# Joining the right half's partial products by DMA in a two-layer encoder kernel, with three shifts in ACT's and DVE's queues

## The chip, the cores and the metric

One Trainium2 chip, of which the kernel uses one core. The metric is the device time of one execution in microseconds (us), lower is better. The core has five engines with a queue each, worked off in order: PE (matmuls), DVE (VectorE, elementwise), ACT (ScalarE, elementwise with a function), POOL (GpSimd, here nearly only an issuer of DMAs) and SP (SyncE, the issuer of the weight DMAs). Times before: 2141.31 us, the median of three runs (2138.82 to 2144.55).

## The reference

A trunk of two layers over 256 tokens of width 2048, all in float32. What matters here, cut short:

```python
for l in range(DEPTH):                      # DEPTH = 2
    mod = cond @ w_ada[l] + b_ada[l]        # (2048) @ (2048, 6*2048)
    sh_a, sc_a, g_a, sh_m, sc_m, g_m = split(mod, 6)
    h = _rmsnorm(x) * (1.0 + sc_a) + sh_a
    proj = h @ w_in[l]
    ...                                     # two kinds of attention, out_a and out_b
    mix = concatenate([out_a, out_b]) @ w_o[l]
    x = x + g_a * mix
    h = _rmsnorm(x) * (1.0 + sc_m) + sh_m
    y = square(relu(h @ w_mlp_in[l])) @ w_mlp_out[l]   # D_FF = 4 * 2048
    x = x + g_m * y
return _rmsnorm(x, final_norm_g)
```

## The kernel before

**Numbers in two parts.** A float32 weight tile is split: ACT rounds it to a high half (`hi`, L158), DVE subtracts to get the low half (`lo`, L161). Each product is three matmuls (high by high, high by low, low by high). Activations are split in the same way (`hidh`/`hidl`, `h`). Raw weight tiles (`raw`) come over SP's queue into a ring of seven buffers, which they share with the adaLN weights (`ada`) and the combined weights (`comb`). There are four `hi` and four `lo` tiles.

**adaLN.** Each of the 192 tiles of `w_ada` is 1 MB; DVE multiplies it with the condition and sums (L387, 2.28 us). `more_ada` spreads these over the program: each stage has a rate, and a load is put in when enough credit is there. RATE_K1 is the rate of layer 1's norm stages.

**The MLP of layer 1.** The hidden width is worked off in four blocks (fb = 0 to 3). In a block, the m loop makes 16 tiles of hidden values (`wides`: L224 and L227, their two banks' sums by ACT L1503 and DVE L1504, then relu and square) and at once multiplies them by the left half of `w_mlp_out` (`seven`: seven products of a 2 by 2 scheme with combined weights, L1335 to L1337, which need mixed hidden values, `sh` and `sl`). The right half follows in `right_by_seven`; it needs the mixed values again, which have been stored to HBM (`mixed`, L1172) and are read back (`sr`, L1181). The left half's products are copied from PSUM by ACT (`part`, L353) and added to HBM tiles by POOL's DMAs (`kept`, L1266), one tile for each product. The right half's products are added (L1262) to four HBM tiles for the four output quarters: a product that counts in several quarters is sent once for each (`IN_BLOCKS`), 15 sends for a block. Sends to one tile wait for one another. In the last block, `last_right` computes the right half directly, reads the eight left products and the four right tiles (L1114) back, multiplies the latter by the gate row (`add_rows`: DVE L1119, then a DMA that adds to x, L1120), and finishes with the final norm. The gate row of the MLP is made in that block as well (`gate`: PE transpose, ACT, two DMAs on POOL).

**Rows and squares.** In the output projection and in the last MLP block, the output comes in four columns of 512 (`rows`, L318 to L321). After each, DVE does `yg` (L1425, times the gate row) and `x` (L1427), and ACT squares x for the next norm (`squares`, L1441).

**Queries and values.** In layer 1's attention, `up_q` makes queries and copies them on ACT (`qn`, L353), `up_v` splits the value weights `w_uv`; the scores (L1676) need the queries.

**What sets the order.** A list scheduler gives each engine its order: among the instructions whose inputs it holds to be ready it takes the one written first. So an instruction may stand in a queue far ahead of its place in the code, and once there it holds up all behind it until its inputs are there. Temporary tiles of 128 by 512 (hidden values, mixed values, copies, sums) come out of one pool of 40 buffers (`u`).

Of the kernel before, what the change touches and what calls it, by code (L numbers as in the profile page):

```python
# [69 lines left out]
def consts():  # L70
# [24 lines left out]
WHOLE = 6  # L95


RATE_A0, RATE_V, RATE_A1, RATE_A2, RATE_K, RATE_K1, RATE_M0 = 1.1, 1.6, 0.7, 1.0, 0.6, 0.4, 1.0
RATE_M3 = 0.75
RATE_S, RATE_R, RATE_E = (0.1, 0.2), (0.8, 0.2), 0.0  # L100
RAWS = 7
IN_BLOCKS = {
    1: ((0, 2), (0, 3), (1, 2), (1, 3)), 2: ((0, 2),), 3: ((0, 3),), 4: ((1, 2),),
    5: ((0, 3), (1, 3)), 6: ((0, 3), (1, 2), (1, 3)), 7: ((1, 2), (1, 3)), 8: ((1, 3),),
}
FILL = "0|1|2|3||||rlm"


class Trunk:
# [213 lines left out]
    def rows(self, src, xs, c, last=False):  # L323

        pss = [self.bank("pr") for _ in range(2)]
        for kq in range(2 if last else 4):
            if last and kq == 1:
                self.first_squares()
            self.rows_by_k(pss, self.weights(src[c, kq]), xs, kq)
        if last:  # L330
            self.quiet = True
            w = [self.weights(src[c, kq]) for kq in (2, 3)]
            for t in range(2):
                for kq in (2, 3):
                    self.rows_by_k(pss, w[kq - 2], xs, kq, (t,))
        return pss
# [13 lines left out]

    def copy(self, ps, name, scale=1.0):
        t = self.u(name)
        self.nc.scalar.activation(t, ps, AF.Copy, scale=scale)  # L353
        return t


# [61 lines left out]
    def setup(self):  # L418
        nc, io, cp = self.nc, self.io, self.cp
        self.ada_plan()  # L420
        self.cond = cp.tile([P, D], F32, name="cond")
        ck = cp.tile([P, NK], F32, name="ck")
        self.pos = cp.tile([P, T + 8], I32, name="pos")
        self.vec = cp.tile([P, NVEC], F32, name="vec")
        self.K = cp.tile([P, NCONST], F32, name="K")
        for t, name, q in ((ck, "ck", nc.scalar), (self.vec, "vec", nc.sync), (self.pos, "pos", nc.scalar),
                           (self.K, "consts", nc.sync)):
            q.dma_start(t, io[name])
        xt = [[None, None], [None, None]]
        for h in range(2):  # L430
            for t in range(2):
                xt[t][h] = self.wp.tile([P, D // 2], F32, tag=("hi", "lo")[h], name=self.name("xt"), bufs=4)
                q = nc.scalar if (h, t) == (1, 0) else nc.sync
                ins = q.dma_start(xt[t][h], io["x"][t, :, D // 2 * h : D // 2 * h + D // 2])
                if q is nc.scalar:
                    issued = ins
        self.eps = cp.tile([P, 1], F32, name="eps")
        nc.gpsimd.memset(self.eps, EPS)
        self.ones = cp.tile([P, P], F32, name="ones")
        nc.gpsimd.memset(self.ones, 1.0)  # L440
        self.ident = cp.tile([P, P], F32, name="ident")
        make_identity(nc, self.ident)
        self.behind(nc.scalar.activation(ck, ck, AF.Silu), issued)
        nc.scalar.activation(self.s("root", 1), ck[:, :1], AF.Sqrt, bias=self.eps, scale=0.0)
        for j in range(4):
            c = slice(512 * j, 512 * j + 512)
            ps = self.bank("pc").rearrange("p a b -> p (a b)")
            for i in range(4):
                col = ck[:, 4 * j + i : 4 * j + i + 1].broadcast_to([P, P])
                nc.tensor.transpose(ps[:, i * P : i * P + P], col, self.ident)  # L450
            if j % 2:
                cond_dve = nc.vector.tensor_copy(self.cond[:, c], ps)
            else:
                cond_act = nc.scalar.activation(self.cond[:, c], ps, AF.Copy)
        self.bias_setup(cond_dve, cond_act)
        self.x = cp.tile([P, NK, T], F32, name="x")
        self.xr = self.x.rearrange("p (a b) c -> p a (b c)", a=2)
        tot = self.sp.tile([P, 2, 2], F32, tag="s22", name="xsq")
        for h in range(2):
            for t in range(2):  # L460
                junk = self.bias[:, 2 * t : 2 * t + 2].rearrange("p a b c -> p (a b c)")
                ins = nc.scalar.activation(junk, xt[t][h], AF.Square, accum_out=tot[:, h, t : t + 1])
                self.behind(ins, cond_act)

        def turn(n, after=None, later=False):
            h, p = n // 4, n % 4
            ps = self.bank("px")
            for i in range(2):
                c = (2 * p + i) * P
                for t in range(2):  # L470
                    nc.tensor.transpose(ps[:, i, t * P : (t + 1) * P], xt[t][h][:, c : c + P], self.ident)
            k = 8 * h + 2 * p

            def copy(after):
                ins = nc.scalar.activation(self.x[:, k : k + 2], ps, AF.Copy)
                if after is not None:
                    self.behind(ins, after)

            return copy if later else copy(after)

        return tot, turn
# [407 lines left out]
    def layer(self, l, acc=None):  # L889
# [28 lines left out]
        else:  # L918
            cqr = [self.joined(banks[i : i + 2], self.u("cqr")) for i in (0, 2)]
            ckr = self.joined(banks[4:], self.u("ckr"))  # L920
        q = []
        cq, ckv = [], []
        kk, qn, kn, qr, vm, a, at, v, o = [], [], [], [], [], [], [], [], []
        self.mo = []
# [17 lines left out]

        def up_q(b):
            qn.extend(self.copy(ps, "qn", ms) for ps in self.small(io["w_uq"][l, b], cq, 4))

        def up_r():
            if l:
# [3 lines left out]
            qr.extend([self.rope_q(x)] * 2 for x in raw)  # L951

        def up_v():
            w = self.weights(io["w_uv"][l])
            for cg in range(2):
                pss = [self.bank("pv") for _ in range(2)]
                self.tokens_by_k(pss, [[z[:, 512 * cg : 512 * cg + 512] for z in y] for y in w], ckv, True, True)
                vm.append([self.copy(ps, "vm") for ps in pss])
# [163 lines left out]
    def block_by_seven(self, l, fb, h, banks):  # L1122
# [2 lines left out]
        hid, pairs, sums, stored = [], [], [None] * 7, {}  # L1125
        plain = len(banks)
        end = fb == NFB - 1
        self.rate = RATE_S[l]
        for m in range(0, plain, 2):
            hid += self.relu2(self.joined(banks[m : m + 2], self.t("sum")))  # L1130
        for m in range(plain, NK, 2):
            both = self.t("sum")
            for j in range(2):
                src = io["w_m11"][NK * fb + m + j - 6] if l else io["w_m10"][NK * fb + m + j - 12]
                ps = self.wides([src], h)[0]
                self.join(ps, both[:, j])
                if len(pairs) > 1:
                    pairs[-2][j]()
            r = self.relu(both)
            parts = self.split(r, "hid")  # L1140
            hid += parts
            mixed = self.mixed(r)
            if l and not end and m >= NK // 2:
                stored[m // 2] = self.stored(mixed)
            pairs.append(self.seven(io[f"w_ms{l}"][fb, m // 2], parts, mixed, sums, m == plain, m == NK - 2))
            if end and m == 2:
                self.gate(l, 5)
        for pair in pairs[-2:]:
            for f in pair:
# [35 lines left out]
    def right_by_seven(self, fb, hid, plain, stored, light):  # L1185
# [9 lines left out]
        begun = [[self.bank("pr") for _ in range(2)] for _ in range(2)]  # L1195
        mixed = {}
        n = NK // 4
        for q in range(n):
            if q > 1:
                mixed[n + q - 2] = self.again(stored[n + q - 2])  # L1200
            self.both_by_k(self.weights(io["w_mr"][fb, q]), hid, 2 * q, begun, q == n - 1, False)
            if light:
                light.pop(0)()
        for f in light:
            f()
        self.keep_product(8, begun[1][1])
        sums = [None, begun[0][0], begun[1][0], begun[0][1], None, None, None]
        for q in range(n, 2 * n):
            if q + 2 < 2 * n:
                mixed[q + 2] = self.again(stored[q + 2])  # L1210
            parts = hid[2 * q : 2 * q + 2]
            for f in self.seven(io["w_mr"][fb, q], parts, mixed[q], sums, q == n, q == 2 * n - 1, (2, 3, 4)):
                f()
        for i in (1, 2, 3, 5, 7, 6, 4):
            self.keep_product(i, sums[i - 1])

    def keep_product(self, i, ps):

        t = self.copy(ps, "part")
        for z in IN_BLOCKS[i]:  # L1220
            self.keep_tile(z, t)

    def last_right(self, hid, sums):

# [6 lines left out]
            for i in group:  # L1231
                op(acc[i], sums[i - 1], acc[i], ALU.add)

        def rows(c):
            for t in range(2):
                self.add_rows(acc[t, c], t, c)

        light = [
            lambda: add(3, 5), lambda: add(7, 6, 4), lambda: rows(2),
            lambda: halves.extend(self.merged(acc)), lambda: rows(3),  # L1240
            lambda: done(halves[0], 0), lambda: done(halves[1], 1),
        ]
        self.read_kept(acc, list(range(1, 9)) + [(t, c) for c in (2, 3) for t in range(2)])
        add(1, 2)
        pss = [self.bank("pr") for _ in range(2)]
        for kq in range(4):
# [182 lines left out]
    def updates(self, pss, c, last=False):  # L1429

        for t in range(2):
            self.update(pss[t].rearrange("p a b -> p (a b)"), t, c)
            if last:
                self.squares(t, c)

    def squares(self, t, c):

# [361 lines left out]
```

## Time and profile before

| | us |
|---|---|
| median of three runs | 2141.31 |
| the profiled execution's own time | 2141.52 |
| its span, first to last instruction | 2139.6 |
| granted TensorE clock | 0.999 |

Where the time goes, by stage; PE and DVE are busy times from a table by windows:

| stage | from to (us) | length | PE busy | DVE busy |
|---|---|---|---|---|
| layer 0: output projection | 325 to 400 | 75 | 73.05 | 64.79 |
| layer 1: attention norm | 1100 to 1147 | 47 | 45.77 | 44.77 |
| layer 1: output projection | 1340 to 1441 | 101 | 101.00 | 81.43 |
| layer 1: MLP norm | 1441 to 1480 | 39 | 38.76 | 37.30 |
| MLP block 0 | 1480 to 1614 | 134 | 134.00 | 121.58 |
| block 1: m loop | 1614 to 1742 | 128 | 126.61 | 114.71 |
| block 1: right half | 1742 to 1789 | 47 | 44.38 | 39.28 |
| block 2: m loop | 1789 to 1916 | 127 | 126.89 | 109.77 |
| block 2: right half | 1916 to 1959 | 43 | 42.70 | 37.22 |
| block 3: m loop | 1959 to 2087 | 128 | 128.00 | 110.89 |
| last right half and final norm | 2087 to 2139 | 52 | 44.24 | 45.46 |

A row of a timeline reads: start, duration, engine, line, operation, output and input tile, and in brackets the idle time ahead of it and what ended it. A row of waits reads: engine, tile, line, what it waited for, then the total, the number of times and the longest. An engine that is busy all the time in a stage sets that stage's length; idle time of another engine costs nothing by itself.

### The profile page before, as it was taken

To read this page: it belongs to the slowest core of one execution; us is meant where nothing else is said; L and a number is where in the kernel's file an instruction comes from. 1 tells how busy PE (TensorE), PEld (TensorE's weight loads), DVE (VectorE), ACT (ScalarE), POOL (GpSimd) and SP (SyncE) were. 2 spreads that over 40 slices of the span, in tenths; PEclk is the share of its full clock that TensorE was granted. 3 is DMA by queue.
4 is the path that set the end of the run, shared out by engine and by line. 5 is a ranking of instruction groups with operands and counts; after the bars stand their busy time and mean duration, and the time that the engine had idled before them with its cause. 6 is when DMAs were issued, how large, how long until landed. Compare 5 with 4: busy or idle time off the path is not lost.

```text
span 2139.6 us, 30063 instructions
## 1 busy us (share of the span) xinstructions
PE 2107.5 (98%) x11327; PEld 1821.2 (85%) x11327; DVE 1854.9 (87%) x2515; ACT 1287.6 (60%) x1904; POOL 136.1 (6%) x202
## 2 busy tenths in 40 slices
PE   7999999999999999999999999999999999999998
PEld 6899888898888888888889998888888888888886
DVE  8889888989799888879978897889988997898898
ACT  6555663564466566646454576647667666676674
POOL 0000000000000100111000000000022022012110
PEclk9999999999999999999999999999999999999999
DMA  9999898789965965899978877877689699679864
GB/s 396 423 386 341 320 352 352 283 316 405 383 218 189 372 226 211 296 404 381 388 261 319 305 288 282 298 302 266 225 309 324 223 302 285 224 228 311 252 228 148
DMA packets 110674, 643.04 MB, mean 301 GB/s; under 512 B 12800, under 2 KB 13248, under 8 KB 43712
## 3 DMA queue, kind: packets, MB, share of 16 engines
q1 hardware_dynamic: 85536, 586.41, 72.0%
q0 software_dynamic: 24272, 53.52, 10.2%
q8 instruction: 88, 1.44, 0.3%
q10 hardware_dynamic: 720, 1.19, 0.2%
q14 instruction: 58, 0.48, 0.1%
HBM read 602.25 MB, written 35.68 MB: 298 GB/s over the span
## 4 chain that ended last, share of the span: by engine, by line
PE 89%; DVE 4%; DMA 4%; issue 2%; ACT 1%; POOL 0%; SPq 0%; ACTq 0%; DVEq 0%; POOLq 0%
PE ps L224 19%; PE ps L227 10%; PE pr L318 7%; PE pr L321 7%; PE pr L319 7%; PE pp L1336 3%; PE pp L1337 3%; PE pp L1335 3%; PE pk L267 3%; DMA ada<-in_w_ada 2%; PE pk L201 2%; PE pk L205 2%; PE pk L204 2%; DVE lo L161 2%; PE pk L291 2%
## 5 line engine op out<-in xcount | busy, mean ns | idle before, releaser
L158 ACT ACTIVATE hi<-raw 128x1024 fp32r<-128x1024 f32 (+2 forms) x714 | 707.1, 1003 | 469.5 <-PE pr L319 127.2
L161 DVE TENSOR_TENSOR lo<-raw,hi 128x1024 fp32r<-128x1024 f32 (+2 forms) x714 | 807.7, 1150 | 175.7 <-ACT hi L158 107.3
L387 DVE SCALAR_TENSOR_TENSOR ada<-ada,cond 128x2048 f32<-128x2048 f32 x192 | 438.3, 2285 | 13.8 <-DMA ada<-in_w_ada 12.8
L224 PE MATMUL ps<-h,hi 128*128 128x512 f32 x1856 | 442.1, 391 | 0.9 <-DVE sum L1504 0.4
L224 PEld LDWEIGHTS ps<-h,hi 128*128 128x128 f32 x1856 | 343.8, 188 | 77.5 <-DVE sum L1504 6.7
L227 PEld LDWEIGHTS ps<-h,lo 128*128 128x128 f32 x1856 | 236.4, 191 | 8.1
L227 PE MATMUL ps<-h,lo 128*128 128x256 f32 x1856 | 238.9, 283 | 0.0
L318 PE MATMUL pr<-hi,hidh 128*128 128x512 f32 x448 | 174.4, 389 | 0.1
L319 PE MATMUL pr<-hi,hidl 128*128 128x512 f32 x448 | 174.3, 389 | 0.0
L161 DVE TENSOR_TENSOR lo<-comb,hi 128x1024 fp32r<-128x1024 f32 x114 | 138.8, 1220 | 8.0 <-ACT hi L158 3.6
L158 ACT ACTIVATE hi<-comb 128x1024 fp32r<-128x1024 f32 x114 | 120.2, 1055 | 30.3 <-PE pp L1337 12.3
L321 PE MATMUL pr<-lo,hidh 128*128 128x512 f32 x448 | 111.4, 389 | 0.0
L318 PEld LDWEIGHTS pr<-hi,hidh 128*128 128x128 f32 x448 | 84.1, 188 | 18.0 <-ACT hi L158 0.5
L321 PEld LDWEIGHTS pr<-lo,hidh 128*128 128x128 f32 x448 | 84.0, 188 | 17.6 <-DVE lo L161 0.2
L319 PEld LDWEIGHTS pr<-hi,hidl 128*128 128x128 f32 x448 | 84.1, 188 | 17.4
L201 PE MATMUL pk<-h,hi 128*128 128x256 f32 x320 | 90.4, 285 | 0.2 <-ACT h L722 0.2
L205 PE MATMUL pk<-h,lo 128*128 128x256 f32 x320 | 90.5, 283 | 0.0
L204 PE MATMUL pk<-h,hi 128*128 128x256 f32 x320 | 90.5, 283 | 0.0
L1262 POOL DMA_DIRECT2D kept<-part x76 | 67.0, 989 | 332.0 <-ACT part L353 257.4
L1503 ACT ACTIVATE sum<-ps 128x256 f32<-128x256 f32 x110 | 41.8, 383 | 75.5 <-PE ps L227 74.3
L267 PE MATMUL pk<-hf,w 128*128 128x256 f32 x384 | 83.9, 379 | 0.0
L267 PEld LDWEIGHTS pk<-hf,w 128*128 128x128 f32 x384 | 72.6, 190 | 10.2 <-ACT hf L694 0.4
(307 smaller groups left out, 3844.3 us busy)
## 6 DMA issues: line engine op xcount, KB each, us to landing
ada<-in_w_ada SPq DMA_DIRECT2D x192, 1024.0 KB, 7.5
raw<-in_w_m SPq DMA_DIRECT2D x166, 1024.0 KB, 7.5
raw<-in_w_ms SPq DMA_DIRECT2D x48, 1024.0 KB, 6.2
raw<-in_w_o SPq DMA_DIRECT2D x32, 1024.0 KB, 7.1
kept<-part POOLq DMA_DIRECT2D x100, 256.0 KB, 9.2
raw<-in_w_mr SPq DMA_DIRECT2D x24, 1024.0 KB, 6.4
raw<-in_w_m SPq DMA_DIRECT2D x24, 768.0 KB, 5.8
raw<-in_w_dv SPq DMA_DIRECT2D x16, 1024.0 KB, 5.0
```

The source lines that it names most:

```text
L158: ins = self.nc.scalar.activation(hi, v, AF.Copy)
L161: ins = self.nc.vector.tensor_tensor(lo, v, hi.bitcast(F32), ALU.subtract)
L201: ins = mm(ps, hi, x[0], start=first, stop=False, skip_group_check=shared)
L204: mm(ps, hi, x[1], start=False, stop=False, skip_group_check=shared)
L205: self.last_mac = mm(ps, lo, x[0], start=False, stop=last, skip_group_check=shared)
L224: mm(ps.rearrange("p a b -> p (a b)"), part(w, k, 0), x[2], start=k == 0, stop=False)
L227: mm(ps[:, 0], part(w, k, 1), x[0], start=False, stop=k == nk - 1)
L267: self.nc.tensor.matmul(ps, v, whole[k], start=first, stop=last, skip_group_check=True)
L318: mm(ps, xh[:, c], part(i, 0), start=kq == 0 and i == 0, stop=False)
L319: mm(ps, xl[:, c], part(i, 0), start=False, stop=False)
L321: self.last_mm = mm(ps, xh[:, c], part(i, 1), start=False, stop=kq == 3 and i == 3)
L387: ins = nc.vector.scalar_tensor_tensor(w, w, 1.0, self.cond, ALU.mult, ALU.mult, accum_out=acc[:, i : i + 1])
```

## The change

- The right half's eight products get HBM tiles of their own (`("r", i)`): 8 sends for a block instead of 15, and no two of a block to one tile.
- At the start of block 3, `right_steps` reads these eight tiles into SBUF, and eight DMAs on POOL add one SBUF tile to another (`IN_ORDER`, L1225 of the changed program). Then the four quarters are multiplied by the gate row and added to x, in the code at m = 12 and 14 of block 3 instead of in `last_right`.
- The last pair of mixed values of a block stays in SBUF: 6 instead of 8 stores and reads for a block, and the reads are written one step earlier.
- The gate row is made in block 2 instead of block 3.
- RATE_K1 goes from 0.4 to 0.3.
- In the output projection and the last MLP block the squares of x of columns 0 to 2 are written behind the second weights of the next column.
- In layer 1, the split of the value weights is written behind the first copy of the queries.

```diff
--- before.py
+++ after.py
-RATE_A0, RATE_V, RATE_A1, RATE_A2, RATE_K, RATE_K1, RATE_M0 = 1.1, 1.6, 0.7, 1.0, 0.6, 0.4, 1.0
+RATE_A0, RATE_V, RATE_A1, RATE_A2, RATE_K, RATE_K1, RATE_M0 = 1.1, 1.6, 0.7, 1.0, 0.6, 0.3, 1.0
...
-IN_BLOCKS = {
-    1: ((0, 2), (0, 3), (1, 2), (1, 3)), 2: ((0, 2),), 3: ((0, 3),), 4: ((1, 2),),
-    5: ((0, 3), (1, 3)), 6: ((0, 3), (1, 2), (1, 3)), 7: ((1, 2), (1, 3)), 8: ((1, 3),),
-}
+IN_ORDER = ((6, 1), (2, 1), (7, 6), (4, 7), (6, 5), (3, 6), (5, 7), (5, 8))
...
         for kq in range(2 if last else 4):
+            w = self.weights(src[c, kq])
+            if kq == 1:
+                self.late_squares()
             if last and kq == 1:
                 self.first_squares()
-            self.rows_by_k(pss, self.weights(src[c, kq]), xs, kq)
+            self.rows_by_k(pss, w, xs, kq)
...
         def up_q(b):
             qn.extend(self.copy(ps, "qn", ms) for ps in self.small(io["w_uq"][l, b], cq, 4))
+            after_queries.append(self.last_copy)
...
         def up_v():
-            w = self.weights(io["w_uv"][l])
+            w = self.weights(io["w_uv"][l], order=(after_queries[0], None) if l else None)
...
         end = fb == NFB - 1
+        right = self.right_steps() if l and end else []
...
                     pairs[-2][j]()
+                if m and right and (len(right) > 4 or m >= NK - 4):
+                    right.pop(0)()
...
             if l and not end and m >= NK // 2:
-                stored[m // 2] = self.stored(mixed)
+                stored[m // 2] = mixed if m == NK - 2 else self.stored(mixed)
...
-            if end and m == 2:
+            if l and fb == NFB - 2 and m == 2:
                 self.gate(l, 5)
...
+        mixed[2 * n - 1] = stored[2 * n - 1]
         for q in range(n):
-            if q > 1:
-                mixed[n + q - 2] = self.again(stored[n + q - 2])
+            if q:
+                mixed[n + q - 1] = self.again(stored[n + q - 1])
...
-        self.keep_product(8, begun[1][1])
+        self.keep(("r", 8), begun[1][1])
         sums = [None, begun[0][0], begun[1][0], begun[0][1], None, None, None]
         for q in range(n, 2 * n):
-            if q + 2 < 2 * n:
-                mixed[q + 2] = self.again(stored[q + 2])
...
         for i in (1, 2, 3, 5, 7, 6, 4):
-            self.keep_product(i, sums[i - 1])
-
-    def keep_product(self, i, ps):
-
-        t = self.copy(ps, "part")
-        for z in IN_BLOCKS[i]:
-            self.keep_tile(z, t)
+            self.keep(("r", i), sums[i - 1])
+
+    def right_steps(self):
+
+        acc = {}
+        self.read_kept(acc, [("r", i) for i in (1, 6, 2, 7, 4, 5, 3, 8)])
+        add = lambda i, j: self.nc.gpsimd.dma_start(acc["r", i], acc["r", j], accum_op=ALU.add)
+        out = {2: (0, 2), 4: (1, 2), 3: (0, 3), 5: (1, 3)}
+        return [lambda p=p: add(*p) for p in IN_ORDER] + [
+            lambda i=i, tc=tc: self.add_rows(acc["r", i], *tc) for i, tc in out.items()]
...
-        def rows(c):
-            for t in range(2):
-                self.add_rows(acc[t, c], t, c)
-
...
-        self.read_kept(acc, list(range(1, 9)) + [(t, c) for c in (2, 3) for t in range(2)])
+        self.read_kept(acc, range(1, 9))
...
             self.update(pss[t].rearrange("p a b -> p (a b)"), t, c)
-            if last:
+            if last and c == 3:
                 self.squares(t, c)
+            elif last:
+                self.later.append((t, c))
+
+    def late_squares(self):
+
+        for t, c in self.later:
+            self.squares(t, c)
+        self.later = []
```

`copy` also notes its last instruction (`last_copy`), and `setup` begins with an empty list `later`.

What this does to the queues is shown at three places. Lines shift by a few: L1119 of before is L1121, L1120 is L1122, L1504 is L1514, L1345 to L1347 are L1347 to L1349, L161 is L158 (the low half), L727 is L728 and L719 is L720.

**DVE, block 3, second step of the m loop.** `sum` is the sum behind a wide, `comb` the combined weights and mixed values, `lo` a low half, `acc` a tile with the right half's joined products. Before:

```order
L1504 SCALAR_TENSOR_TENSOR sum_18327<-ps_18328,sum_18327 128x256
L161 TENSOR_TENSOR lo_18450<-raw_18443,hi_18449 128x1024
L1320 TENSOR_TENSOR sl_18324<-comb_18318,sh_18323 128x512
L1345 TENSOR_TENSOR comb_18646<-raw_18644 128x1024
L1346 TENSOR_TENSOR comb_18646<-raw_18644,comb_18646 128x512
L161 TENSOR_TENSOR lo_18501<-raw_18494,hi_18500 128x512
L161 TENSOR_TENSOR lo_18508<-raw_18494,hi_18507 128x1024
L1504 SCALAR_TENSOR_TENSOR sum_18327<-ps_18373,sum_18327 128x256
L1347 TENSOR_TENSOR comb_18646<-raw_18644,comb_18646 128x512
L1314 TENSOR_TENSOR comb_18425<-relu_18418 128x128
L1315 TENSOR_TENSOR comb_18425<-relu_18418 128x128
L1316 TENSOR_TENSOR comb_18425<-comb_18425,relu_18418 128x128
```

The same place in the changed program:

```order
L1347 TENSOR_TENSOR comb_18625<-raw_18623 128x1024
L1121 TENSOR_TENSOR acc_18194<-acc_18194,bias 128x512
L158 TENSOR_TENSOR lo_18478<-raw_18471,hi_18477 128x512
L158 TENSOR_TENSOR lo_18485<-raw_18471,hi_18484 128x1024
L1514 SCALAR_TENSOR_TENSOR sum_18309<-ps_18356,sum_18309 128x256
L1348 TENSOR_TENSOR comb_18625<-raw_18623,comb_18625 128x512
L1121 TENSOR_TENSOR acc_18198<-acc_18198,bias 128x512
L1349 TENSOR_TENSOR comb_18625<-raw_18623,comb_18625 128x512
L1121 TENSOR_TENSOR acc_18196<-acc_18196,bias 128x512
L1316 TENSOR_TENSOR comb_18409<-relu_18402 128x128
L1317 TENSOR_TENSOR comb_18409<-relu_18402 128x128
L1318 TENSOR_TENSOR comb_18409<-comb_18409,relu_18402 128x128
```

Three of the four multiplies stand here, though the code has them at m = 12 and 14; the first stands ten rows earlier, directly behind the sum of the second wide of the block (that of 1972.18 us in the trace of before). Nothing else in DVE's order differs here.

**POOL, start of block 3.** Before, the queue ends its 15 sends of block 2 here and goes on with the gate row:

```order
L1262 DMA kept_14968<-part_18212 128x512
L1262 DMA kept_14970<-part_18217 128x512
L1262 DMA kept_14778<-part_18212 128x512
L1414 DMA gate_18434<-modT_18436 16x128
L1416 DMA bias<-gate_18434 128x2048
```

In the changed program the sends are followed by eight reads (tiles 18186 to 18200 hold products 1, 6, 2, 7, 4, 5, 3, 8 in this order; the first needs product 1, the second product 6, the fifth product 4, which is the block's last send), and then:

```order
L1225 DMA acc_18188<-acc_18186 128x512
L1225 DMA acc_18190<-acc_18186 128x512
L1225 DMA acc_18192<-acc_18188 128x512
L1122 DMA x<-acc_18190 128x512
L1225 DMA acc_18194<-acc_18192 128x512
L1225 DMA acc_18188<-acc_18196 128x512
L1225 DMA acc_18198<-acc_18188 128x512
L1225 DMA acc_18196<-acc_18192 128x512
L1122 DMA x<-acc_18194 128x512
L1225 DMA acc_18196<-acc_18200 128x512
L1122 DMA x<-acc_18198 128x512
L1122 DMA x<-acc_18196 128x512
```

Each L1225 adds the tile on the right to that on the left. The multiplies above read 18190, 18194, 18198 and 18196, so each stands behind the L1225 rows that write its tile.

**DVE, MLP norm of layer 1.** `ht` and `h` make the normed input, `lo` the weights' low halves. Before:

```order
L161 TENSOR_TENSOR lo_13452<-raw_13445,hi_13451 128x768
L719 SCALAR_TENSOR_TENSOR ht_13481<-xT_13286,mod_95,pn_13247 128x256 x2
L161 TENSOR_TENSOR lo_13493<-raw_13490,hi_13492 128x768
L727 SCALAR_TENSOR_TENSOR h_13482<-ht_13481,mod_93,h_13482 128x256
L161 TENSOR_TENSOR lo_13497<-raw_13490,hi_13496 128x768
L727 SCALAR_TENSOR_TENSOR h_13483<-ht_13481,mod_93,h_13483 128x256
L387 SCALAR_TENSOR_TENSOR ada_13455,macc_98<-ada_13455,cond 128x2048
```

The changed program:

```order
L158 TENSOR_TENSOR lo_13451<-raw_13444,hi_13450 128x768
L387 SCALAR_TENSOR_TENSOR ada_13409,macc_98<-ada_13409,cond 128x2048
L720 SCALAR_TENSOR_TENSOR ht_13479<-xT_13282,mod_95,pn_13243 128x256 x2
L158 TENSOR_TENSOR lo_13491<-raw_13488,hi_13490 128x768
L158 TENSOR_TENSOR lo_13495<-raw_13488,hi_13494 128x768
L728 SCALAR_TENSOR_TENSOR h_13480<-ht_13479,mod_93,h_13480 128x256
L728 SCALAR_TENSOR_TENSOR h_13481<-ht_13479,mod_93,h_13481 128x256
```

The `ada` stands five instructions earlier, and both low halves stand ahead of the first `h`.

More of the change, by code (lines that the diff above doesn't have):

```diff
@@ L352, in copy @@
         t = self.u(name)
-        self.nc.scalar.activation(t, ps, AF.Copy, scale=scale)
+        self.last_copy = self.nc.scalar.activation(t, ps, AF.Copy, scale=scale)
         return t
@@ L920, in layer @@
             ckr = self.joined(banks[4:], self.u("ckr"))
-        q = []
+        q, after_queries = [], []
         cq, ckv = [], []
@@ L1232, in add @@
                 op(acc[i], sums[i - 1], acc[i], ALU.add)
-        def rows(c):
-            for t in range(2):
-                self.add_rows(acc[t, c], t, c)
         light = [
-            lambda: add(3, 5), lambda: add(7, 6, 4), lambda: rows(2),
-            lambda: halves.extend(self.merged(acc)), lambda: rows(3),
+            lambda: add(3, 5), lambda: add(7, 6, 4), lambda: halves.extend(self.merged(acc)),
             lambda: done(halves[0], 0), lambda: done(halves[1], 1),
         ]
-        self.read_kept(acc, list(range(1, 9)) + [(t, c) for c in (2, 3) for t in range(2)])
+        self.read_kept(acc, range(1, 9))
         add(1, 2)
@@ L1432, in updates @@
             self.update(pss[t].rearrange("p a b -> p (a b)"), t, c)
-            if last:
+            if last and c == 3:
                 self.squares(t, c)
+            elif last:
[3 more added lines that the diff above has]
+            self.squares(t, c)
+        self.later = []
     def squares(self, t, c):
```

## The prediction

> **What bounds the kernel now.** The page's first part comes first, then the waits of PE.
>
> ```profile
> PE 2107.5 (98%) x11327; PEld 1821.2 (85%) x11327; DVE 1854.9 (87%) x2515; ACT 1287.6 (60%) x1904; POOL 136.1 (6%) x202
> PE pr L1337 <- DMA sr<-mixed: 2.8, 3, 1.3
> PE pr L318 <- ACT hi L158: 1.9, 2, 1.0
> PE psm L1676 <- ACT qn L353: 1.3, 1, 1.3
> PE pk L291 <- DVE h L727: 1.0, 2, 0.5
> PE pp L1335 <- ACT hi L158: 0.9, 1, 0.9
> ```
>
> PE works 98% of the span, so no more than about 32 us of 2139.6 can be won without removing matmuls, and the change removes none. The wait rows give us in total, times, and the longest. The five rows are those the change can reach, 7.9 us together. DVE at 87% is nearly full, and its queue is strictly in order: whatever stops DVE for longer than its lead over PE stops PE. So each part is judged by two questions: does one of these waits go, and does DVE get a new one?
>
> **The change, part by part.** *Squares later (layer 0, output projection).* A high half (ACT, L158) comes late because ACT stands behind a square that waits for DVE's x, and DVE does an adaLN sum (`ada`) between yg and x:
>
> ```profile
> 350.15 2.28 DVE L387 SCALAR_TENSOR_TENSOR ada<-ada,cond 128x2048 f32<-128x2048 f32 x1
> 352.35 0.69 DVE L1427 TENSOR_TENSOR x<-x,yg 128x512 f32<-128x512 f32 x1
> 353.07 0.63 ACT L1441 ACTIVATE sq<-x 128x512 f32<-128x512 f32 x1 [9.50 <-DVE x L1427]
> 355.04 3.89 ACT L158 ACTIVATE hi<-raw 128x1024 fp32r<-128x1024 f32 x4
> ```
>
> In the changed order ACT's queue is the same here, but DVE does yg, yg, x, x, then the low halves, then `ada`. The squares start about 2.2 us earlier and the wait of `pr L318` goes: −1.9. Elsewhere (layer 0's last block, layer 1's output projection) the low halves now stand behind yg and x, where PE waits for nothing today. Each yg or x ahead of a low half delays it by 0.6 to 0.7 us (the row of 352.35), most of which is slack, as no wait of PE stands there: +0.3 for all six places, bounds 0 and 1.2.
>
> *One `ada` load fewer in layer 1's norm stages.* In the attention norm the second `ada` no longer stands ahead of `h`:
>
> ```profile
> 1127.07 2.28 DVE L387 SCALAR_TENSOR_TENSOR ada<-ada,cond 128x2048 f32<-128x2048 f32 x1
> 1131.47 1.67 PE L291 MATMUL pk<-h,hi 128*128 128x512 f32 x6 [0.53 <-DVE h L727]
> ```
>
> That is −0.5. In the MLP norm it moves the wrong way: from behind an `h` to ahead of one (the order rows of the MLP norm above).
>
> ```profile
> 1457.03 0.86 DVE L719 SCALAR_TENSOR_TENSOR ht<-xT,mod,pn 128x256 f32<-128x256 f32 x2
> 1457.81 0.95 DVE L161 TENSOR_TENSOR lo<-raw,hi 128x768 fp32r<-128x768 f32 x1
> 1458.68 0.48 DVE L727 SCALAR_TENSOR_TENSOR h<-ht,mod,h 128x256 fp32r<-128x256 f32 x1
> 1460.88 1.55 PE L291 MATMUL pk<-h,hi 128*128 128x512 f32 x6
> ```
>
> At 1457.03 DVE now does `ada` (2.2 net), two ht (0.8), two lo (0.87 each), then h (0.48): ready at 1462.3 for a matmul that starts at 1460.88. **+1.4**, bounds 0 and 1.6.
>
> *Query copies ahead of the value weights.* ACT fills all its high halves, then the query copy, and PE's scores wait for that copy:
>
> ```profile
> 1270.21 1.06 ACT L158 ACTIVATE hi<-raw 128x1024 fp32r<-128x1024 f32 x1 [0.88 <-PE pv L305]
> 1271.18 1.07 ACT L353 ACTIVATE qn<-pss 128x512 f32<-128x512 f32 x2
> ```
>
> The copies now come first: −1.3.
>
> *Right half kept apart; last mixed pair stays in SBUF.* Today three reloads stand on POOL's queue behind the partial sum of product 8, which waits 9.4 us for ACT:
>
> ```profile
> 1768.75 0.89 POOL L1262 DMA_DIRECT2D kept<-part  x1 [9.41 <-ACT part L353]
> 1769.32 1.95 POOL L1181 DMA_DIRECT2D sr<-mixed  x3
> ```
>
> In the changed order all reloads stand ahead of it and the last pair is not stored at all: the wait of `pr L1337` goes, −2.8. The stores fall from 15 to 8 per block; nothing but POOL and the u buffers waits for these.
>
> *More `ada` in blocks 0 and 1.* An `ada` directly ahead of the sum that frees the psum bank, with PE drawn to a high half that is not ready, stands once in today's m loops:
>
> ```profile
> 1717.30 2.28 DVE L387 SCALAR_TENSOR_TENSOR ada<-ada,cond 128x2048 f32<-128x2048 f32 x1
> 1719.55 0.50 PE L1335 MATMUL pp<-hi,hidh 128*128 128x512 f32 x1 [0.92 <-ACT hi L158]
> ```
>
> The changed order has the same PE, ACT and DVE sequence twice (blocks 0 and 1): one more, +0.9, bounds 0 and 2. The last `ada` and the gate row at the start of block 2 lie where DVE has idle time (2.32 us in the row of 1974.92 below, one block later).
>
> These terms sum to −1.9 + 0.3 − 0.5 + 1.4 − 1.3 − 2.8 + 0.9 = **−3.9**.
>
> *The sums joined by DMA, and where DVE waits for them.* This is the largest term. DVE's four multiplies L1121 stand among the first steps of block 3 (the order rows of block 3 above), each behind a DMA. Today DVE and PE pass there at:
>
> ```profile
> 1972.18 0.42 DVE L1504 SCALAR_TENSOR_TENSOR sum<-ps,sum 128x256 f32<-128x256 f32 x1
> 1974.92 0.29 DVE L1314 TENSOR_TENSOR comb<-relu 128x128 f32<-128x128 f32 x1 [2.32 <-ACT relu L1512]
> 1985.85 0.29 DVE L1314 TENSOR_TENSOR comb<-relu 128x128 f32<-128x128 f32 x1 [1.57 <-ACT relu L1512]
> 1986.92 1.22 DVE L161 TENSOR_TENSOR lo<-comb,hi 128x1024 fp32r<-128x1024 f32 x1
> 1989.70 0.39 PE L1336 MATMUL pp<-lo,sh 128*128 128x512 f32 x1
> ```
>
> The first multiply comes right after the sum of 1972.18, the fourth right before the comb of 1985.85; the lo of 1986.92 is needed by PE at 1989.70. When are their inputs there? The partial sums of block 2 leave at the same time as now:
>
> ```profile
> 1956.28 3.58 POOL L1262 DMA_DIRECT2D kept<-part  x4 [12.76 <-ACT part L353]
> 1965.89 0.88 POOL L1262 DMA_DIRECT2D kept<-part  x1 [6.03 <-DMA kept<-part]
> kept<-part POOLq DMA_DIRECT2D x4, 256.0 KB, 12.9
> kept<-part POOLq DMA_DIRECT2D x1, 256.0 KB, 12.4
> acc<-kept POOLq DMA_DIRECT2D x2, 256.0 KB, 2.9
> acc<-kept POOLq DMA_DIRECT2D x8, 256.0 KB, 12.9
> x<-acc POOLq DMA_DIRECT2D x4, 256.0 KB, 3.3
> x<-acc POOLq DMA_DIRECT2D x3, 256.0 KB, 12.0
> ```
>
> The last six rows are DMA issues, with the median us from issue to landing: the four stores of 1956.28, the one of 1965.89, the first two and the next eight reads for the last right half (from 2061.07 and 2074.83), the four x additions after 2098 and the three of 1036.37. The queue is shared with the weight stream, and the same 256 KB takes 2.9 us when that is quiet and 12 us when it is not. Today the fifth store lands at 1965.89 + 12.4 = 1978.3. It is queued without a gap, so the sixth and seventh of the changed kernel land near 1979.6 and 1981 (1.3 us apart, an estimate: POOL needs 0.9 for one, a quarter of the 3.58, and the weight stream thins out by then). The reads of products 6 and 4 wait for exactly these two. Eight reads at about 0.55 us each put the first accumulate at **1984**.
>
> From there DVE's fourth multiply is five accumulates deep (6+=1, 7+=6, then 4+=7 with 5 into 6 beside it, 5+=7, 5+=8), and POOL issues each only when the one before has landed. No SBUF-to-SBUF accumulate between two work tiles is in this trace; the nearest row is x<-acc, 3.3 us quiet, 12.0 loaded. I take 3.3, since a DVE that stands still frees no weight buffers and so stops the weight stream, plus 0.6 until POOL's next issue (1965.89 comes that long after its landing). Five links of 3.9 and 1.8 for the issues in between give 21.3: the fourth input is there at 2005.3. The multiply (0.6), the rest of the comb (0.8) and the lo (1.2) follow, so PE gets at 2007.9 what it used at 1989.70: **+18.2** of PE standing still. In general the stall is the start of the chain minus 1965.8. Nothing makes it up later, since PE is the bound, and it can't be negative, since PE waits for nothing there today.
>
> The bounds: with a queue as quiet as the 2.9 row from 1956 on, the stores land by 1964.6, the chain starts at 1967.5 and the stall is 1.7; with links of 5 us in place of 3.3, it is 27.
>
> Sum: 2141.5 (the profiled execution's own time, 2139.6 of span and 1.9 around it) − 3.9 + 18.2 = 2155.8. That execution is 0.2 above the median of the runs shown, so **2155.5**.
>
> The Trainium skill, "DMA: Bandwidth & Descriptors", section on the anatomy of one DMA on the SWDGE path, fits one such transfer as 2.0 us plus bytes over 436 KB per us, 2.6 us for 256 KB. By that rule the links would be 3.2 and no store late, the stall would vanish and the sum would be 2137.4, the near end of the first rival. The trace disagrees: 2.9 us at best, 12.9 beside the weight stream; the same page's section on SWDGE, HWDGE and iDMA says that an engine serves the two kinds of queue in turn, which fits the loaded rows.
>
> **The rivals.** (1) *Quiet queue*, the case that ends not slower: the change halves the stores on this queue, so the sums may be joined nearly by the time DVE asks. The price is 0 to 6: 2137 to 2143. For it: the 2.9 and 3.3 rows. Against: those come where few weights are streamed, and the 12.9 row comes at this very place. It decides if the chain starts before about 1972; from 1976 on the stall outweighs the gains by over 0.3%. (2) *Slow links*: weights already under way keep the queue loaded; 2164. (3) *All small waits go and DVE waits for none*: quiet queue, no new stall at the norm (+1.4) or by `ada` (+0.9): 2141.3 − 6.5 + 0.3 = 2135.1, and 0.1 less for each of the nine waits gone, as the matmul behind one is longer (0.50 at 1719.55, 0.39 at 1989.70): 2134.2. (4) *The squares do nothing*, ACT's order there being unchanged: 1.9 more, inside the range of each case.
>
> **How the numbers follow.** Forecast (2148 to 2160) 0.55; slow links 0.12; quiet queue 0.24, of which 0.03 comes out above 2148; all waits gone 0.09, three quarters of it under 2134.9. A measurement of this kernel can tell about 0.3%, 6.4 us, from no change. So faster 0.07, same 0.23, slower 0.70. The range takes in most of the quiet case and nearly all of the slow one: 2138 to 2164; the forecast's own is 2148 to 2160.
>
> **What would show it.** In the profile of the changed kernel: DVE's L1121 in block 3 with idle time ahead of it that ends with a DMA, PE waiting for DVE's lo some 10 us later, L1225 rows on POOL about 4 us apart, and a slice of low PE near 1985 to 2005. Gone: the waits on sr, on qn, and L318's on hi. New: a short wait of L291 for h near 1461, and a second one of L1335. If L1121 has no idle time ahead of it, the forecast is wrong by its whole largest term.

## The result, and the profile after

| | us |
|---|---|
| before, median of five runs (2138.71 to 2144.55) | 2140.37 |
| after, median of five runs (2169.34 to 2175.14) | 2171.86 |
| ratio | 1.0145, 95% interval 1.0128 to 1.0161 |
| profiled execution after: own time, span, granted clock | 2172.9, 2171.1, 0.991 |

The change costs 31.5 us; about 14 were predicted (2155.5 against 2141.3), and 2171.86 lies above the range. The busy row of the page, the waits of PE and the waits of DVE for a DMA (in all, times, longest), all of the changed kernel:

```profile
PE 2115.3 (97%) x11327; PEld 1827.7 (84%) x11327; DVE 1853.5 (85%) x2515; ACT 1284.9 (59%) x1904; POOL 118.9 (5%) x181
PE pp L1338 <- DVE lo L158: 18.8, 4, 12.8
PE ps L224 <- DVE lo L158: 8.6, 2, 8.4
PE pp L1337 <- ACT hi L155: 1.8, 2, 0.9
PE pk L288 <- DVE h L728: 1.7, 2, 1.3
DVE acc L1121 <- DMA acc<-acc: 29.5, 3, 18.7
```

The waits on `sr`, on `qn` and of the output projection on `hi` are gone. In their place stand 27.4 us of PE waiting for low halves of DVE (L1338 and L224), of which 21.2 fall in block 3 (8.38 and 12.79 in the rows below). DVE itself waits 29.5 us at L1121. DVE does the same work as before (1853.5 us against 1854.9) in a longer span: it lost time standing. POOL's timeline shows the chain it stood behind (start, duration, line, operation, tiles, count, idle before):

```profile
1961.81 4.42 POOL L1264 DMA_DIRECT2D kept<-part  x5 [0.15 <-issue]
1982.96 3.92 POOL L1116 DMA_DIRECT2D acc<-kept  x7 [14.22 <-DMA kept<-part]
1986.86 1.85 POOL L1225 DMA_DIRECT2D acc<-acc  x2
1993.60 0.85 POOL L1225 DMA_DIRECT2D acc<-acc  x1 [4.88 <-DMA acc<-acc]
1997.09 1.77 POOL L1225 DMA_DIRECT2D acc<-acc  x2 [0.62 <-DMA acc<-acc]
2003.84 1.80 POOL L1225 DMA_DIRECT2D acc<-acc  x2 [4.98 <-DMA acc<-acc]
2013.16 0.87 POOL L1225 DMA_DIRECT2D acc<-acc  x1 [6.63 <-DMA acc<-acc]
```

From one link's issue to the next: 6.7, 3.5, 6.8 and 9.3 us. DVE, SP and PE at the same place:

```profile
1975.39 0.42 DVE L1514 SCALAR_TENSOR_TENSOR sum<-ps,sum 128x256 f32<-128x256 f32 x1
1994.52 0.69 DVE L1121 TENSOR_TENSOR acc<-acc,bias 128x512 f32<-128x512 f32 x1 [18.72 <-DMA acc<-acc]
1999.41 4.37 SPq L174 DMA_DIRECT2D raw<-in_w_m  x2
2011.44 0.69 DVE L1121 TENSOR_TENSOR acc<-acc,bias 128x512 f32<-128x512 f32 x1 [7.08 <-DMA acc<-acc]
2016.45 0.69 DVE L1121 TENSOR_TENSOR acc<-acc,bias 128x512 f32<-128x512 f32 x1 [3.72 <-DMA acc<-acc]
1997.13 2.07 PE L224 MATMUL ps<-h,lo 128*128 128x256 f32 x8 [8.38 <-DVE lo L158]
2019.07 0.80 PE L1338 MATMUL pp<-lo,sh 128*128 128x512 f32 x1 [12.79 <-DVE lo L158]
2019.66 0.63 PE L1339 MATMUL pp<-hi,sl 128*128 128x512 f32 x1
```

The matmul that PE reached at 1989.70 before is now reached at 2019.07, 29.4 us later. Of this 3.2 had been lost earlier (the sum of 1972.18 stands at 1975.39), so block 3's wait costs 26.2, and the slow matmuls behind it more (0.63 us each; they took 0.39 before). The matmuls between the two waits are slow as well (a granted clock of 0.50 from 1996 to 2004), but that costs nothing extra: DVE stands for the chain behind them, until 2011.44 and again until 2016.45.

Two stalls that nobody forecast made the earlier loss. In block 2's right half:

```profile
1923.65 0.60 ACT L353 ACTIVATE part<-pp 128x512 f32<-128x512 f32 x1 [4.95 <-DMA kept<-part]
1926.25 1.23 DVE L158 TENSOR_TENSOR lo<-raw,hi 128x1024 fp32r<-128x1024 f32 x1 [4.92 <-ACT hi L155]
1940.88 1.23 DVE L1347 TENSOR_TENSOR comb<-raw 128x1024 f32<-128x1024 f32 x1 [2.73 <-DMA raw<-in_w_mr]
1944.02 0.50 PE L1338 MATMUL pp<-lo,sr 128*128 128x512 f32 x1 [3.48 <-DVE lo L158]
1944.73 0.63 PE L1337 MATMUL pp<-hi,sr 128*128 128x512 f32 x1
```

ACT's copy waits for the landing of a send, that is, for a free `u` buffer; DVE waits for ACT, the next load of these weights goes out late, and PE stands 3.48 us. SP's issues of the two loads, first in the changed kernel and then in the kernel before:

```profile
1920.76 13.55 SPq L174 DMA_DIRECT2D raw<-in_w_mr  x2
1922.02 8.95 SPq L177 DMA_DIRECT2D raw<-in_w_mr  x2
```

The second load ends its issue at 1934.3 instead of 1931.0.

At the start of block 2, SP's queue, DVE and PE:

```profile
1772.08 0.33 SPq L371 DMA_DIRECT2D ada<-in_w_ada  x1
1793.21 0.33 SPq L1371 DMA_DIRECT2D cond<-in_fg  x1
1795.92 0.33 SPq L174 DMA_DIRECT2D raw<-in_w_ms  x1
1811.82 1.22 DVE L1347 TENSOR_TENSOR comb<-raw 128x1024 f32<-128x1024 f32 x1 [3.75 <-DMA raw<-in_w_ms]
1818.31 0.50 PE L1338 MATMUL pp<-lo,sh 128*128 128x512 f32 x1 [2.10 <-DVE lo L158]
```

The last `ada` tile is now loaded between the first weights of block 2; a weight lands late, and PE stands 2.10 us.

### The profile page after: what moved, and what is told of

It reads as the page before. It is cut to its first block, busy times and chain, and to the rows that moved or that the text cites. A ratio compares the mean times of both kernels' runs of the same rounds, so it can differ in the third digit from the quotient of the medians.

```text
span 2171.1 us, 30006 instructions
## 1 busy us (share of the span) xinstructions
PE 2115.3 (97%) x11327; PEld 1827.7 (84%) x11327; DVE 1853.5 (85%) x2515; ACT 1284.9 (59%) x1904; POOL 118.9 (5%) x181
## 3 DMA queue, kind: packets, MB, share of 16 engines
q8 instruction: 89, 1.46, 0.3%
## 4 chain that ended last, share of the span: by engine, by line
PE 82%; issue 8%; DVE 4%; DMA 4%; ACT 1%; POOL 1%; SPq 0%; POOLq 0%; DVEq 0%; ACTq 0%
PE ps L221 15%; PE ps L224 8%; PE pr L315 7%; PE pr L316 7%; PE pr L318 7%; PE pk L264 3%; PE pp L1338 3%; PE pp L1339 3%; PE pp L1337 3%; PE pk L198 2%; PE pk L202 2%; PE pk L201 2%; DVE lo L158 2%; PE pv L302 2%; PE pv L300 2%
## 5 line engine op out<-in xcount | busy, mean ns | idle before, releaser
L158 DVE TENSOR_TENSOR lo<-raw,hi 128x1024 fp32r<-128x1024 f32 (+2 forms) x714 | 807.4, 1150 | 187.0 <-ACT hi L155 110.0
L387 DVE SCALAR_TENSOR_TENSOR ada<-ada,cond 128x2048 f32<-128x2048 f32 x192 | 438.2, 2284 | 13.2 <-DMA ada<-in_w_ada 12.2
L224 PEld LDWEIGHTS ps<-h,lo 128*128 128x128 f32 x1856 | 238.0, 192 | 17.4 <-DVE lo L158 9.3
L224 PE MATMUL ps<-h,lo 128*128 128x256 f32 x1856 | 241.1, 284 | 8.6 <-DVE lo L158 8.6
L158 DVE TENSOR_TENSOR lo<-comb,hi 128x1024 fp32r<-128x1024 f32 x114 | 138.8, 1220 | 8.3 <-ACT hi L155 3.9
L1338 PE MATMUL pp<-lo,sh 128*128 128x512 f32 x189 | 74.3, 397 | 14.9 <-DVE lo L158 14.9
```

The lines of the kernel that those rows point to most:

```text
L158: ins = self.nc.vector.tensor_tensor(lo, v, hi.bitcast(F32), ALU.subtract)
L224: mm(ps[:, 0], part(w, k, 1), x[0], start=False, stop=k == nk - 1)
L387: ins = nc.vector.scalar_tensor_tensor(w, w, 1.0, self.cond, ALU.mult, ALU.mult, accum_out=acc[:, i : i + 1])
L1338: nc.tensor.matmul(ps, x[0], wl, start=False, stop=False)
```

## The experiments

The kernel before was timed beside each; differences below are to its median in the same job (2141.65 for the first four, 2141.53 for the next four, 2142.28 for the last).

**1. Multiplies held back** (the changed kernel):

```diff
+        self.last_join = self.nc.vector.scalar_tensor_tensor(t, ps[:, 1], scale, t, ALU.mult, ALU.add)
...
+        if held:
+            self.behind(ins, self.last_join)
```

> The changed kernel with one difference: the four multiplies by the gate row are held behind the sum of the m step at which the code has them (steps 13 to 16 of block 3 instead of 2 to 4); the eight reads and the eight accumulates stay. Theory A (DVE stands in its queue behind the accumulate chain, and PE with it): the 29.5 us of DVE waiting for DMA in block 3 go, with the slow clock after them; 2144 to 2148 us. Rival B (the reads and accumulates themselves cost the time, by the u buffers or the DMA queue, wherever the multiplies stand): 2165 or more.

Measured: 2148.87, ratio 1.0032 (1.0021 to 1.0042), +7.2 instead of +31.5. No wait at L1121 is left. But the chain itself is slower than in the changed kernel; POOL here:

```profile
1984.21 1.85 POOL L1227 DMA_DIRECT2D acc<-acc  x2
1995.38 0.85 POOL L1227 DMA_DIRECT2D acc<-acc  x1 [9.31 <-DMA acc<-acc]
2003.23 1.76 POOL L1227 DMA_DIRECT2D acc<-acc  x2 [7.00 <-DMA acc<-acc]
2013.05 1.79 POOL L1227 DMA_DIRECT2D acc<-acc  x2 [8.07 <-DMA acc<-acc]
2025.24 0.88 POOL L1227 DMA_DIRECT2D acc<-acc  x1 [10.40 <-DMA acc<-acc]
```

Beside a weight stream that never stops, a link takes 7.9 to 12.2 us. From the first issue to the last 41 us pass, and it costs almost nothing (+7.2 against the +5.6 of run 2, which has no such chain), because DVE asks only at 2058.6. So it is the place of the multiplies that costs.

**2. The right half joined in HBM again**; pair in SBUF, gate in block 2, the other edits left:

```diff
-            self.keep(("r", i), sums[i - 1])
+            self.keep_product(i, sums[i - 1])
...
```

> The changed kernel with the right half's sums sent to four HBM tiles again, 15 sends for a block, no reads or accumulates at the start of block 3; the last mixed pair still stays in SBUF, the gate row is still made in block 2. Theory A: the wait in block 3 goes, 2140 to 2147; the wait of ACT's third part copy in block 2's right half (5.0 us for a u buffer) stays, since the mixed pair holds the buffers. Rival B2 (that wait is due to the sends being apart): it goes too, and the time is under 2140.

Measured: 2147.20, 1.0025 (1.0014 to 1.0036), +5.6. The wait in block 3 is gone, the one at the end of block 2 stays:

```profile
ACT part L356 <- DMA kept<-part: 10.1, 4, 5.1
1948.46 0.79 PE L1340 MATMUL pp<-lo,sr 128*128 128x512 f32 x1 [4.85 <-DVE lo L161]
```

So that stall isn't made by the eight separate tiles. More `u` buffers weren't tried.

**3. The last mixed pair stored and read back as before** (the changed kernel):

```diff
-                stored[m // 2] = mixed if m == NK - 2 else self.stored(mixed)
+                stored[m // 2] = self.stored(mixed)
...
```

> The changed kernel with the last mixed pair stored to HBM and read back as before. If the pair that stays in SBUF takes the u buffers that ACT's part copies need: the 5.0 us wait of the copy and the 3.6 us wait of PE in block 2's right half go, with the slow clock after it, 2164 to 2168, less 0 to 3 us if the reloads are late again as before (waits of PE for sr up to 2.8 us). Rival: the copy's wait stays, 2172. The block 3 wait of DVE (29 us) stays in both.

Measured: 2170.91, 1.0133 (1.0118 to 1.0148), +29.3. ACT's wait and the stall of 1944 are gone, and a wait for the read is back:

```profile
1779.82 0.80 PE L1340 MATMUL pr<-hi,sr 128*128 128x512 f32 x1 [2.66 <-DMA sr<-mixed]
DVE acc L1121 <- DMA acc<-acc: 31.0, 3, 19.5
```

So the pair made the stall of block 2 and saved one of similar size in block 1, and the wait in block 3 doesn't come from it. The rows show this, not the time, which lies only 1 us under the changed kernel's 2171.86.

**4. RATE_K1 back to 0.4** (the changed kernel, this number alone).

> The changed kernel with RATE_K1 at 0.4 as before. If the adaLN loads that slid into blocks 0 to 2 cost what the prediction said: the 1.3 us wait of L288 for h in the MLP norm and one of the two 0.9 us waits of L1337 go, and the 2.3 us wait of PE in block 2 (weights of 1 MB landing late behind ada and the final gain's load) goes or shrinks; the 0.5 us wait in the attention norm comes back: 2166 to 2170. Rival: the loads don't matter, 2172. The block 3 wait stays in both.

Measured: 2167.59, 1.0116 (1.0100 to 1.0133), +25.9. SP's queue has no `ada` and no `cond` at the start of block 2 any more, and the stalls of 1818 and 1459 and one of the two before a high half are gone; a wait of PE of 1.46 us at 1767.41 is new. By the times the moved `ada` loads cost 5.6 us, give or take 5, as both kernels' times are known to about 3.5.

**5. The two small edits alone** (the kernel before with late squares and early query copies).

> The kernel before, with two of the change's edits alone: the squares behind the next high halves, and the query copies ahead of the value weights; right half, gate, pair and ada as before. Theory A (everything that the change lost lies in the right half's sums apart, the pair that stays in SBUF and the moved ada loads; these two edits only gain): 3 to 4 us faster than before, about 2138 (squares -1.9 +0.3, norms about -0.5, query copies -1.3), with no PE stall behind the query copies and none over 1 us that the kernel before has not. Rival B (part of the loss comes from these two edits, which put every later step at another point of the weight stream): 0 to 5 us slower than before.

Measured: 2139.54, 0.9988 (0.9979 to 0.9997): 2.0 faster, 0.6 to 4.5 by the interval. Both waits that these edits were to remove are gone; the reads stay late:

```profile
PE pr L1342 <- DMA sr<-mixed: 2.7, 2, 1.4
```

A gain, smaller than expected and barely clear of none. It is the one version whose interval lies on the faster side of the kernel before.

**6. The right half apart and the gate in block 2, alone on the kernel before.**

> The kernel before, with the right half's eight sums apart and the gate row in block 2 alone; squares, query copies, pair and ada as before. Theory A (DVE's early multiplies wait for the accumulates whatever else is done): 23 to 31 us slower than before, about 2165 to 2172; DVE acc L1121 <- DMA acc<-acc about 28 to 31 us in 3 or 4 waits, PE stalls of 8 to 10 and of 12 to 15 us in block 3. Rival B (the wait came of the 3 us that the kernel was already late and of the weights that the stall at the end of block 2 had put off): under 15 us slower, since here block 2 has no stall of the pair.

Measured: 2169.93, 1.0130 (1.0117 to 1.0144), +28.4. Waits of DVE and PE:

```profile
DVE acc L1121 <- DMA acc<-acc: 29.9, 3, 19.1
PE pp L1339 <- DVE lo L158: 13.8, 3, 13.1
PE ps L224 <- DVE lo L158: 8.9, 2, 8.8
```

Here nothing was late before: the first link goes out at 1982.87 instead of 1986.86, and the wait is as long. The rival falls.

**7. The gate row in block 3 again** (the changed kernel).

```diff
-            if l and fb == NFB - 2 and m == 2:
+            if end and m == 2:
```

> The changed kernel with the gate row made in block 3 again, as before; nothing else undone. The multiplies need the gate row, so the four of them then stand after block 3's fifth, fifth, fifth and seventh sum instead of its second, third, fourth and fourth. Theory A (the place of the multiplies in DVE's order decides, and the wait shrinks by what DVE does before it): the first multiply comes some 10 us later, so the DVE wait falls from 29.5 to about 14 to 20 us, the time to 2158 to 2165. Rival B (the accumulates go on only when the weight stream ends or PE stands, so that they come later as the multiplies do): 2169 to 2174, the wait unchanged near 29 us.

Measured: 2171.59, 1.0139 (1.0124 to 1.0154), +30.1. This was forecast wrong. The time is the rival's, but not for its reason, as DVE's wait and POOL show (rows of an execution of 2177.15 us):

```profile
DVE acc L1121 <- DMA bias<-gate: 25.6, 1, 25.6
2009.73 1.75 POOL L1225 DMA_DIRECT2D acc<-acc  x2 [7.09 <-DMA acc<-acc]
2014.73 1.75 POOL L1225 DMA_DIRECT2D acc<-acc  x2 [3.25 <-DMA acc<-acc]
2019.69 0.87 POOL L1225 DMA_DIRECT2D acc<-acc  x1 [3.21 <-DMA acc<-acc]
2020.23 0.84 POOL L1416 DMA_DIRECT2D gate<-modT  x1
2023.45 0.58 POOL L1418 DMA_DIRECT2D bias<-gate  x1 [2.37 <-DMA gate<-modT]
```

The multiplies did move back, but the gate row's two DMAs now stand behind the accumulates on POOL, and each accumulate holds POOL until the one before has landed. The multiplies wait for the whole chain all the same. So this run says nothing on the place of the multiplies, and it shows what moving the gate into block 2 is needed for. It also has the link without weight loads: SP issues none between 2000.27 and 2031.17, and the links from 2009.73 and from 2014.73, of two accumulates each, take 5.0 us each.

**8. Three undone at once** (multiplies held, pair stored, RATE_K1 0.4).

> The changed kernel with three things at once: the multiplies held behind the sum of their step, the last mixed pair stored and read back as before, and the earlier rate of ada loads. Theory A (three separate causes, which add): from 2148.9 of the held kernel, without the stall at the end of block 2 (3.6 and about 2 of slow clock), without the late weights at its start (1.7) and the stalls of moved ada (2.5), but with the read of the pair late again (2.8 and about 2 of slow clock): 2140 to 2146. Rival B (they share one cause, the load on the queues, and one opened shifts to another): 2147 to 2152.

Measured: 2140.94, 0.9993 (0.9984 to 1.0002), −0.6: theory A's range. The pair and the `ada` rate are worth 7.8 us together (this run against run 1, each known to about 2), which is clear of noise. That 7.2 − 2.2 − 5.6 gives the −0.6 to a tenth is luck, as the 2.2 and 5.6 (runs 3 and 4) are uncertain by about 5 each. What is left of the change, sums by DMA included, is no faster than the two small edits alone (2139.54 beside the same kernel before): the joined sums bring nothing that shows, and two short waits of 0.52 and 1.04 us at the end are new.

**9. Reads of the mixed pairs one step earlier, with the two small edits:**

```diff
-            if q > 1:
-                mixed[n + q - 2] = self.again(stored[n + q - 2])
+            if q:
+                mixed[n + q - 1] = self.again(stored[n + q - 1])
...
```

> The kernel before with the two gaining edits (squares later, query copies first) and, new, the three first reads of the stored mixed pairs one step of the right half earlier, so that no send of a sum and fewer weights stand ahead of them. Theory A (the reads are late because they are issued late; 2.7 us of PE waits on sr in the kernel with the two edits alone, and about 0.6 of slow clock): these waits fall below 0.5 us, the time to 2135 to 2138, 3 to 6 us faster than before. Rival B (the earlier reads hold their buffers longer, and ACT's copies or DVE's low halves wait instead, as in the changed kernel at the end of block 2): 2138 to 2144, with ACT or DVE waits on DMA kept<-part or on weights in their place.

Measured: 2142.15, 1.0001 (0.9991 to 1.0010). The waits on `sr` are gone, and the rival came:

```profile
ACT part L356 <- DMA kept<-part: 9.5, 2, 5.2
1938.31 0.79 PE L1341 MATMUL pp<-lo,sr 128*128 128x512 f32 x1 [3.24 <-DVE lo L161]
```

Both ways of holding one more pair of `u` buffers there, the pair kept in SBUF and a read issued early, end in such a stall.

**The sum of the parts.** Right half and gate +28.4 (run 6), pair +2.2 (31.5 less 29.3), `ada` rate +5.6 (31.5 less 25.9), small edits −2.0 (run 5): 34.2 for a measured 31.5. Runs 5 and 6 are known to about ±2 and ±3, the two differences only to about ±5, so the parts fit within their noise and no closer claim can be made; the pair's 2.2 is within noise by itself. That −2.0 + 2.2 + 5.6 = 5.8 meets run 2's 5.6 rests on the same two differences.

## Why the prediction was right in its sign and half its size

- **The largest term, DVE's wait for the joined sums: right in mechanism, too small.** Predicted 18.2, measured 26.2. The start of the chain was right: 1984 predicted, 1986.9 measured in a kernel that was 3.2 us late there. The step that failed is the link: "I take 3.3, since a DVE that stands still frees no weight buffers and so stops the weight stream". From the first issue to the fourth input 29.6 us passed (1986.86 to 2016.45), not 21.3. The first link ran beside the reads and a second accumulate and took 6.7 us. And DVE doesn't stand still throughout: between its first and third multiply it works, frees buffers, and SP sends two weight tiles from 1999.41 on; the two links beside them took 6.8 and 9.3 us, against 5.0 for run 7's links of two accumulates without weights. DVE's own work isn't what slowed the 9.3: it stood for 7.08 of it. Only the links of one accumulate without weights (3.5 and 3.3 us) were as short as the prediction's 3.9. The bound of 27 for links of 5 us held, and rival (2), slow links, named the cause but not its size. Run 1 shows links of 7.9 to 12.2 us if the weights never stop.
- **Not in the sum: slow matmuls after a pause.** PE at 0.39 us for a matmul before and 0.63 after the long waits: about 1.9 us behind 2019 and 1.7 behind 1944, worked out from the clocks in the last section as the share of the time that the clock was short of 1.00.
- **Pair in SBUF: the gain was right, its price was missing.** The wait on `sr` went (−2.8). "Nothing but POOL and the u buffers waits for these" named the buffers and didn't follow them: the pair holds two, ACT's copies wait for the next, and 3.48 us of PE and the slow matmuls behind them are the price. Runs 2, 3 and 9 show it from three sides.
- **More `ada`: half right.** The norm's wait (+1.4) came as forecast, 1.26 us of idle time at 1459.44, and the second wait before a high half too (+0.9). "The last `ada` and the gate row at the start of block 2 lie where DVE has idle time" failed: it weighed DVE's 2.3 us and left out SP's queue, where the `ada` load and the final norm's row stand among the weights. Cost: 2.1 us of PE. In run 4 the waits at 1459 and 1818 and one before a high half are gone, and one of 1.46 us is new.
- **Squares and query copies: the waits went as forecast.** The sum of the two edits, with run 5's older `ada` rate, was −2.9; measured −2.0.
- **The ledger.** The prediction's net +14.3, the missing 8.0 of the chain, 1.9 and 1.7 of slow matmuls, 3.5 and 2.1 of the two unforeseen stalls: 31.5, against 31.4 between the two profiled executions. That it closes so well is partly luck, as single stalls move by some tenths from run to run.

## What to carry to other kernels

When an in-order engine that is nearly full gets an instruction behind a chain of dependent DMAs, price a link by the rows beside the traffic that will run then, other links of the chain included, and ask where a scheduler has put the waiting instruction: the chain cost 26 us where DVE came to it at 1975.8 and almost nothing where DVE came to it at 2058.6. A tile that stays on chip instead of a store and a read has a price, the buffers it holds, and its payer is whoever allocates next from that pool. An added load is priced twice, on the engine that consumes it and in the queue that issues it.

## What the hardware showed that was not expected

The granted clock (the figure before the DMA share) in windows of the changed kernel, first behind the 2.10 us wait at 1818, then behind the 3.48 us wait at 1944:

```profile
1818.00:1820.00 2.00, 1.69 (x7) 1.42 (x8) 2.00 (x4) 2.00 (x4) 0.00 (x0) 1.00 1.02 414
1944.00:1946.00 2.00, 1.98 (x5) 1.59 (x6) 2.00 (x3) 0.00 (x0) 0.00 (x0) 0.60 0.00 0
1946.00:1948.00 2.00, 2.00 (x6) 1.57 (x5) 2.00 (x3) 1.06 (x1) 0.00 (x0) 0.55 0.63 127
1948.00:1950.00 2.00, 2.00 (x10) 1.66 (x9) 1.05 (x2) 1.57 (x2) 0.00 (x0) 1.00 1.05 414
2020.00:2024.00 4.00, 4.00 (x13) 3.13 (x12) 4.00 (x5) 2.48 (x3) 0.00 (x0) 0.64 0.06 10
```

After 2.10 us of standing still the clock is full; after 3.48 it is about half for some 4 us of resumed work, at a cost of 1.7 us. The length of a wait alone doesn't decide it. Run 3's 2.66 us had the slow matmul as well (0.80 us), and in run 2 a wait of 2.09 us at 1819.78 was followed by a clock of 0.50 from 1821.78 to 1823.78; in the kernel before, a wait of 2.83 us at 34.01 left it at 1.00. So these traces give no limit: a pause of 2 to 3 us sometimes costs PE up to 2 us more than itself. The Trainium skill, "TensorE: Matmul & The Clock Gate", Part 1 on the HAM clock gate, has the clock halved after an idle window of about 3.4 us and full again after as much sustained work; the recovery of about 4 us agrees, and the drops after 2.66 and 2.09 us came earlier than it says. Behind run 2's wait of 4.85 us the clock stayed at 0.50 longer, from 1948 to 1954.

An accumulate of 256 KB from SBUF to SBUF took 3.3 us from issue to DVE's use where no weight load was issued (2013.16 to 2016.45), 5.0 us from link to link where two ran at a time without one (run 7), and 7.9 to 12.2 us from link to link beside the weight stream.
